# Weight tiles split ahead in attention, and activation sums by accumulating DMAs, in a hybrid decoder layer

## The chip, the cores and the metric

One Trainium2 chip, one of its cores. The metric is the device time of one launch in microseconds; the number compared is the median of runs. The engines are named as in the profile: PE (TensorE matmuls), PEld (its weight loads), DVE (VectorE), ACT (ScalarE), POOL (GpSimd) and SP (SyncE, which here only issues DMAs). Each engine works through its own instruction queue in order.

## The reference

One layer over 1024 tokens with width 1024, all in float32:

```
h = x
h = h + 0.5 * rmsnorm(swiglu(rmsnorm(h), ffn1_w_gu, ffn1_w_down))       # D_FF 2816
m = stick_breaking_attention(16 heads of 64) | mamba-2 SSD(16 heads), joined, @ w_out (2048 x 1024)
h = h + rmsnorm(m)
c = cross_attention(rmsnorm(h), 256 memory tokens, 4 heads of 256)       # wq, wkv, wo
h = h + rmsnorm(c)
h = h + 0.5 * rmsnorm(swiglu(rmsnorm(h), ffn2_w_gu, ffn2_w_down))
```

## The kernel before, in words

**Arithmetic.** Every float32 operand of a large product is split into a high part (a cast to fp32r, on ACT, line 263) and a low part (source minus high, on DVE, line 265), and each product is three matmuls: high x high, high x low, low x high (`mm3`). The tokens are two halves of 512 columns (`hh` 0 and 1), so one matmul has 128 rows and 512 columns.

**Weight tiles.** `wtile` loads a 128 x 1024 weight tile through a raw buffer (`wraw`, two of them), splits it into `whi` and `wlo` (three buffers of each tag), and for a tile named by a string such as `"q 3"` or `"out 5"` also stores both parts to DRAM (`khi`, `klo`, by POOL's queue), so that the second use loads the two parts instead of splitting again. `wstream` keeps one tile ahead. Forty-three other tiles (among them all q/k/v tiles of attention and `out 8` to `out 15`) are split during the first feed-forward by `prepare` and later loaded as `dwhi`/`dwlo`. `"out 0"` to `"out 7"` (the attention half of the output projection) are split when `mix_out` first uses them, and `"q 0"` to `"q 7"` when `xattn` first uses them.

**Stages in order.** First feed-forward up (0 to about 447 us of the profiled span) and down (`down_first`, to about 673), SSD (to about 1010), attention with the start of the output projection (to about 1578), the rest of the output projection (`mix_out`, to about 1737), cross-attention (`xattn`, to about 2000), second feed-forward.

**down_first.** The down product is done by Strassen's method: seven products (in the order 1, 5, 2, 6, 3, 7, 4) of quarter matrices, each over 11 blocks of 12 matmuls. `operands(p, b)` makes a block's left and right operands; `taker` makes them five blocks ahead of PE. Raw quarters come into a ring of four raw tiles (`wraw` and `raw2`, two each), and the split parts go to eight `hl` and eight other places. The left operands are sums of quarters of the activations A: p 5 needs A21+A22, p 6 that minus A11, p 3 A12 minus the sum of p 6, p 7 A11-A21. All 44 sums (four products x 11 blocks) are DVE additions of 128 x 512 (line 976). When a product ends, its four banks are added to the result tiles F on DVE (line 976 too), and their squares are summed for the norm (`sumsq`, two accumulators, joined by one more DVE addition on line 384).

**Order.** A planner in the framework puts the instructions of each engine in an order by simulating the program with its own durations; a tile with several buffers is given whichever buffer comes free. The order of PE is fixed by hand (each matmul behind the one before). Work beside the products hangs on `self.later`, a list keyed by a clock that counts PE's matmuls: `post` puts the norm's small matmuls (`cols`, `rows`), the eight `apply` steps of a half and its sums there; `resid` the POOL loads of the residual. Instructions from that list keep the order in which they were written on their engine.

**attention.** Eight head pairs. `inproj(p)` projects q, k and v of a pair (six products of 24 matmuls) while `units` works on the pair before: scores, a sigmoid on ACT, a scan on DVE, transposes, and products with the values. POOL does only memsets. At the end, `before` loads and scales the SSD half for the output projection, and `mix_row` makes the rows of a norm: its low tile lies in the buffer that also takes the result (`rpre1`), which the last projection still reads.

Of the kernel before, what the change touches and what calls it, by code (L numbers as in the profile page):

```python
# [18 lines left out]
P = 128  # L19
S = 1024  # L20
H = 512
KT = 8
# [24 lines left out]
class Kern:  # L47
    def __init__(self, nc, tc, ap):
        self.nc, self.tc, self.ap = nc, tc, ap
        self.uid = 0  # L50
        self.clock = 0.0
        self.prev = None
        self.floating = None
        self.pins = []
        self.later = []
        self.inlater = False
        self.more = False
        self.kept = {}

    def nm(self, base):  # L60
        self.uid += 1
# [112 lines left out]
    def wtile(self, src, eng=None):  # L174

        nc = self.nc
        key = None
        if isinstance(src, str):
            key, src = src, self.split_once(src)
        if isinstance(src, tuple):  # L180
            hi = self.t(self.wp, [P, KT, P], F32R, "whi", bufs=3)
            lo = self.t(self.wp, [P, KT, P], F32R, "wlo", bufs=3)
            for o, x in zip((hi, lo), src):
                nc.sync.dma_start(out=o.bitcast(F32), in_=x.bitcast(F32))
            return hi, lo
# [10 lines left out]
        return hi, lo  # L196

    def split_once(self, key):
        if key in self.kept:
# [138 lines left out]
        if r2 is not None:  # L338
            self.kp(nc.vector.tensor_tensor(out=c, in0=c, in1=r2, op=ALU.mult))

    def rms_rows(self, c, home, behind=False):

        nc = self.nc
        nb = c.shape[1]
        cs = self.t(self.tp, [P, 16], F32R, "cs", bufs=1)
        ch, cl = cs[:, 0:nb], cs[:, 4 : 4 + nb]
        self.kp(nc.vector.tensor_copy(ch, c))
        self.kp(nc.vector.tensor_tensor(out=cl, in0=c, in1=ch.bitcast(F32), op=ALU.subtract))
        dg = self.t(self.tp, [P, 4, P], F32R, "dg", bufs=1)
        if isinstance(home, tuple):  # L350
            pool, tag = home
            low = self.t(pool, [P, 4, P], F32R, tag, bufs=1)[:, 0:nb, :]
# [54 lines left out]
    def post(self, hh, gname, r2, gnext=None, out=None, step=None, spread=True, pins=(23000, 28000), accs=None, tail=None, times=None):  # L407
# [36 lines left out]
        def presum(d):  # L444
            if d == 0:
                accs2.extend(self.new_accs())
            self.sumsq(accs2, d, self.F[hh][d])

        T0 = self.clock
        if step is None:  # L450
            with self.pinned(T0 + t1):
                cols()
# [166 lines left out]
    def up_phase(self, sp, sp2, wgu, gpre, act_d, bank, load, plain, sizes, rw=None, begin=None, between=None):  # L619
# [162 lines left out]
        def seven(f):  # L782
# [32 lines left out]
            with self.urgent():  # L815
                nc.vector.tensor_tensor(out=t0, in0=t0, in1=b, op=ALU.mult)
            with self.urgent():
                self.emptied = nc.vector.tensor_tensor(out=e, in0=e, in1=b, op=ALU.subtract).ins  # L818
# [19 lines left out]
        def up(f, hh, t, w):  # L838
            ps = self.proj_now(w, hh)
            with self.urgent():  # L840
                nc.vector.tensor_tensor(out=t, in0=t, in1=ps, op=ALU.mult)
            store(f, hh, t)

        if begin:
# [98 lines left out]
    def seven_tools(self, sp, rw, sums_d=None):  # L943
# [31 lines left out]
        def add(o, x, y, op):  # L975
            return nc.vector.tensor_tensor(out=o, in0=x, in1=y, op=op)

        def taker(operands, ahead):
            order = [(p, b) for p in (1, 5, 2, 6, 3, 7, 4) for b in range(NFF // 2)]
            made, taken = [], [0]  # L980
# [26 lines left out]
    def down_first(self, sp, rw, wdn, act_d, gpost, gnext):  # L1007
# [10 lines left out]
            pool, tag, bufs = spot  # L1018
            return self.t(pool, [P, H], F32, tag, bufs=bufs)

        def operands(p, b):
            a, w = (lambda hh, k: act_d[b][hh][:, k, :]), (lambda k, dh: wdn[b, dh, k])
            tile = place() if p == 1 and b < 2 else self.t(sp, [P, 2, H], F32R, "hl", bufs=8)
            if p == 1:
                x, y = load(a(0, 0), w(0, 0))
                d = wdif[b] = held((self.xp, f"xl{int(b > 3)}", KT + 1))
                nc.sync.dma_start(out=d, in_=w(0, 1))
                o = parts(tile, x), parts(place(), y)
                t = wsum[b] = held(spots[b])
                i = add(t, d, y, ALU.subtract)  # L1030
                if b > 1:
                    self._after(i.ins, self.emptied)
                return o
            if p == 5:
                x, y = load(a(1, 0), a(1, 1))
                k = keep[b] = held((self.xp, f"xh{b // KT}{b % KT}", 1))
                add(k, x, y, ALU.add)
                return parts(tile, k), parts(place(), wsum[b])
            if p == 2:
                x, y = load(a(0, 1), w(1, 0))  # L1040
# [4 lines left out]
                add(wdif[b], z, wdif[b], ALU.subtract)  # L1045
                return o
            if p == 6:
                x, y = load(a(0, 0), w(1, 0))
                add(keep[b], keep[b], x, ALU.subtract)
                o = parts(tile, keep[b]), parts(place(), wsum[b])  # L1050
                add(wsum[b], wsum[b], y, ALU.subtract)
                return o
            if p == 3:
                x, y = load(a(0, 1), w(1, 1))
                add(x, x, keep.pop(b), ALU.subtract)
                return parts(tile, x), parts(place(), y)
            if p == 7:
                x, y = load(a(0, 0), a(1, 0))
                add(x, x, y, ALU.subtract)
                return parts(tile, x), parts(place(), wdif.pop(b))  # L1060
            (x,) = load(a(1, 1))
            return parts(tile, x), parts(place(), wsum.pop(b))

        take = taker(operands, 5)
        four = range(4)
        F = [[self.F[hh][4 * dh : 4 * dh + 4] for dh in range(2)] for hh in range(2)]

# [12 lines left out]
            self.more = False  # L1080

        accs = [self.new_accs(), None]

        def squares(hh, dh, i0):
            with self.urgent():
# [14 lines left out]
        ps = banks(0)  # L1100
        product(ps)
        for i in four:
            update(F[1][0][i], F[1][0][i], ps[i])
        for i in four:
            add(F[1][1][i], F[1][1][i], F[1][0][i], ALU.add)
        self.resid(0, 2700, 22000)
        ps = banks(1)
        product(ps)
# [17 lines left out]
        ps = banks(1)  # L1126
        product(ps, n=NB - 4)
        units = [take() for _ in range(4)]
        accs[1] = [held((rw, tag, 1)) for tag in ("bh", "bl")]
        squares(1, 1, 0)  # L1130
        for i in four:
            blocks(ps, units, i, False, True)
            update(F[1][0][i], F[1][0][i], ps[i], ALU.subtract)
# [518 lines left out]
    def attention(self):  # L1652
        nc, ap = self.nc, self.ap
        with self.pools("at", ["o", "a"], []) as (op, sp, pp):
# [51 lines left out]
            def inproj(p):  # L1706
# [48 lines left out]

                h0, h1 = slice(0, H), slice(H, S)
                wq = next(W)
                qevac((yield from self.proj(wq, 0)), h0)
                qevac((yield from self.proj(wq, 1)), h1)
                wk = next(W)  # L1760
                kevac(evac((yield from self.proj(wk, 0)), 0), h0)
                wv = next(W)
                tv = []
# [33 lines left out]
                    late.pop()()  # L1797

            def mix_row(i):
                product = self.rms_rows(self.norm_c[i][:, 0:4], (self.rp, f"rpre{i}"), True)  # L1800
                return lambda: self.mix_r.append(product())

            def scores(p, a, c):
# [277 lines left out]
    def xattn(self):  # L2081
# [3 lines left out]
        with self.pools("xf", ["a", "b"], []) as (sp, sp2, pp):  # L2085
# [48 lines left out]
            def values(s):  # L2134
                VH, VL = V[s]
                if s == 0:
                    self.place(sp, 128)
# [285 lines left out]
```

## Time and profile before

| | us |
|---|---|
| three runs | 2637.93, 2638.12, 2639.47 |
| median | 2638.12 |
| profiled execution | 2645.18 |
| its span, first to last instruction | 2643.4 |
| granted clock, mean over the span | 0.992 |

| engine | busy us | share of span |
|---|---|---|
| PE | 2576.9 | 97% |
| PEld | 2135.0 | 81% |
| DVE | 1983.2 | 75% |
| ACT | 1262.9 | 48% |
| POOL | 530.8 | 20% |

A row of the page that groups instructions reads: line, engine, operation, output tile <- input tiles, shapes, count, busy time, mean of one in ns, idle time of the engine just ahead of them and what ended it. A matmul's own duration overlaps the next one's; the distance of two starts is what it costs.

### The profile page before, as it was taken

The numbers are of one execution on the slowest core, as the hardware profiler recorded it, in microseconds if no ns is written. First come the engines' busy times: TensorE is split into PE (matmuls) and PEld (weight loads), VectorE is DVE, ScalarE is ACT, GpSimd is POOL, SyncE is SP. The second block draws the span as 40 slices with busy tenths as digits, with TensorE's granted clock in tenths as the row PEclk, the third lists the DMA queues.
The fourth block names the chain that finished last, engine by engine and source line by source line (L and its number), as shares of the span: only waits on it lengthen the run. The fifth ranks groups of instructions, "written<-read, shape, count | busy, mean of one in ns | idle before, by whom it ended". The sixth has DMA issues, their size and how long they took to land.

```text
span 2643.4 us, 36454 instructions
## 1 busy us (share of the span) xinstructions
PE 2576.9 (97%) x12598; PEld 2135.0 (81%) x12598; DVE 1983.2 (75%) x3085; ACT 1262.9 (48%) x2276; POOL 530.8 (20%) x660
## 2 busy tenths in 40 slices
PE   8999999999999999999999998999999999999998
PEld 6788888887777778888888787887878788888887
DVE  7888787888678774777777777775448989895675
ACT  7544443545367783445554445254445433333432
POOL 1555552001100000000000001122012555542000
PEclk9999999999999999999999999999999999999999
DMA  5688887754721226433434458777667455555976
GB/s 209 238 308 302 304 282 252 255 193 158 259 79 45 71 70 196 115 99 108 109 108 115 146 178 323 252 274 252 218 230 272 167 187 203 195 180 210 347 276 218
DMA packets 225241, 528.87 MB, mean 200 GB/s; under 512 B 28064, under 2 KB 35104, under 8 KB 225056
## 3 DMA queue, kind: packets, MB, share of 16 engines
q1 hardware_dynamic: 190432, 419.56, 48.2%
q0 software_dynamic: 27424, 93.87, 9.8%
q10 hardware_dynamic: 7200, 13.11, 1.3%
q8 instruction: 99, 1.62, 0.3%
q14 instruction: 86, 0.70, 0.1%
HBM read 353.41 MB, written 152.04 MB: 191 GB/s over the span
## 4 chain that ended last, share of the span: by engine, by line
PE 79%; DVE 9%; DMA 6%; ACT 3%; issue 2%; POOL 1%; SPq 0%; DVEq 0%; ACTq 0%; POOLq 0%
PE mm L138 45%; PE dn L138 24%; PE z L138 2%; PE ms L138 2%; PE tr L141 2%; PE y L138 1%; PE ms L141 1%; DMA wraw<-act 1%; DMA raw<-act 1%; DVE hl L265 1%; DVE wlo L265 1%; PE seg L138 1%; DMA blk<-h 1%; DVE whi L265 0%; DMA oraw<-mix 0%
## 5 line engine op out<-in xcount | busy, mean ns | idle before, releaser
L138 PE MATMUL mm<-xh,whi 128*128 128x512 f32 x1288 | 511.5, 406 | 11.1 <-ACT xh L270 7.0
L138 PE MATMUL mm<-xh,wlo 128*128 128x512 f32 x1240 | 478.5, 393 | 3.2 <-DVE wlo L265 2.9
L138 PE MATMUL mm<-xl,whi 128*128 128x512 f32 x1188 | 467.8, 394 | 1.0 <-DVE xl L265 0.7
L138 PEld LDWEIGHTS mm<-xh,whi 128*128 128x128 f32 x1288 | 244.1, 189 | 53.6 <-ACT xh L270 6.9
L138 PEld LDWEIGHTS mm<-xh,wlo 128*128 128x128 f32 x1240 | 234.3, 189 | 55.3 <-DVE wlo L265 3.4
L138 PEld LDWEIGHTS mm<-xl,whi 128*128 128x128 f32 x1188 | 225.6, 190 | 34.1 <-DVE xl L265 1.8
L1823 DVE TENSOR_TENSOR_SCAN nb<-nb,begin 128x128 f32<-128x128 f32 (+7 forms) x128 | 171.7, 1352 | 55.0 <-ACT nb L1819 54.4
L1819 ACT ACTIVATE nb<-z,scale 128x128 f32<-128x128 f32 (+2 forms) x192 | 107.8, 580 | 88.8 <-PE z L138 87.7
L263 ACT CAST whi<-wraw 128x1024 fp32r<-128x1024 f32 (+1 forms) x89 | 81.2, 914 | 69.1 <-PE mm L138 39.1
L1856 POOL MEMSET ath<- 128x128 f32 x64 | 13.1, 205 | 499.0 <-PE mm L138 499.0
L265 DVE TENSOR_TENSOR wlo<-wraw,whi 128x1024 fp32r<-128x1024 f32 x61 | 74.4, 1220 | 38.3 <-ACT whi L263 38.0
L138 PE MATMUL dn<-xh,wlo 128*128 128x512 f32 x296 | 101.0, 389 | 0.0
L737 POOL TENSOR_TENSOR wc<-wraw,raw 128x512 f32<-128x512 f32 x57 | 87.5, 1535 | 66.6 <-DVE whi L265 30.7
L737 POOL TENSOR_TENSOR wc<-raw,wraw 128x512 f32<-128x512 f32 x55 | 85.5, 1555 | 66.5 <-DVE wlo L265 31.4
L819 POOL TENSOR_TENSOR ft<-ft,e 128x512 f32<-128x512 f32 x38 | 62.4, 1642 | 144.2 <-DVE e L818 85.7
L650 ACT ACTIVATE ft<-ft 128x512 f32<-128x512 f32 x88 | 55.4, 631 | 75.0 <-DVE ft L649 70.3
L263 ACT CAST ath<-tr 128x512 fp32r<-128x512 f32 (+1 forms) x107 | 58.2, 545 | 67.5 <-PE tr L141 66.1
L138 PE MATMUL dn<-xh,blk 128*128 128x512 f32 x280 | 90.2, 389 | 0.0
L265 DVE TENSOR_TENSOR atl<-tr,ath 128x512 fp32r<-128x512 f32 (+1 forms) x107 | 67.0, 629 | 29.2 <-ACT ath L263 28.9
L138 PE MATMUL dn<-xh,whi 128*128 128x512 f32 x256 | 88.0, 389 | 0.0
L138 PE MATMUL mm<-ath,v 128*128 128x256 f32 x320 | 86.2, 291 | 0.6 <-DVE sq L1838 0.6
L382 DVE TENSOR_TENSOR acc<-acc,sq 128x512 f32<-128x512 f32 x78 | 52.3, 684 | 42.5 <-ACT sq L381 42.2
(586 smaller groups left out, 6667.9 us busy)
## 6 DMA issues: line engine op xcount, KB each, us to landing
whi<-dwhi SPq DMA_DIRECT2D x57, 512.0 KB, 3.4
wlo<-dwlo SPq DMA_DIRECT2D x57, 512.0 KB, 4.2
wraw<-act SPq DMA_DIRECT2D x102, 256.0 KB, 4.4
raw<-act SPq DMA_DIRECT2D x96, 256.0 KB, 4.3
wraw<-in_w_gu SPq DMA_DIRECT2D x44, 512.0 KB, 4.4
raw<-in_w_gu SPq DMA_DIRECT2D x38, 512.0 KB, 4.8
khi<-whi POOLq DMA_DIRECT2D x30, 512.0 KB, 4.6
klo<-wlo POOLq DMA_DIRECT2D x30, 512.0 KB, 6.7
```

The source lines that it names most:

```text
L138: self._pe(self.nc.tensor.matmul(out, lhsT, rhs, start=start, stop=stop, skip_group_check=self.more), cost)
L141: self._pe(self.nc.tensor.transpose(out, src, self.ident if ident is None else ident), 109.0)
L263: self.kp(self.nc.scalar.copy(hi, src))
L265: (eng or self.nc.vector).tensor_tensor(out=lo, in0=src, in1=hi.bitcast(F32), op=ALU.subtract)
L382: self.kp(nc.vector.tensor_tensor(out=accs[i % 2], in0=accs[i % 2], in1=sq, op=ALU.add))
L650: nc.scalar.activation(t, t, AF.Silu)
L737: nc.gpsimd.tensor_tensor(out=t, in0=a, in1=b, op=op)
L819: nc.gpsimd.tensor_tensor(out=t1, in0=t1, in1=e, op=ALU.mult)
L1819: nc.scalar.activation(nb[:, s0:s1], z[:, 0:n], AF.Sigmoid, scale=sc[:, i : i + 1])
L1823: nc.vector.tensor_tensor_scan(out=nb[:, 0:Wd][:, ::-1], data0=nb[:, 0:Wd][:, ::-1], data1=begin[:, S - Wd : S][:, ::-1], initial=0.0, op0 ...
L1856: nc.gpsimd.memset(x[:, 0, :].bitcast(F32), 0.0)
```

## The change

Two parts, which do not touch the same stages.

**Part one.** A new `split_ahead(key)` runs in `inproj(p)`: for `"q 0"` to `"q 6"` (p 1 to 7, when q's tile is taken) and for `"out 0"` to `"out 7"` (every p, when k's tile is taken). It takes a `whi` and a `wlo` buffer of the ring of three, has POOL load the raw tile into `wlo`, casts to `whi` on ACT 6500 ns of PE's clock later, subtracts in place on DVE 1000 ns after that, and stores both by POOL another 1000 ns later. `mix_out` and `xattn` then find these 15 tiles in `kept`. The low tile of the second `mix_row` moves from `rpre1` to an `ev` buffer.

**Part two.** In `down_first`, a new `fetch(p, b)` runs three blocks ahead of `operands` and forms the 44 activation sums by DMA: SP loads the first quarter into its tile, then a POOL DMA with `accum_op=ALU.add` adds the second. The up phase stores the second token half with its sign turned, so that only additions are needed, and three later updates of F change sign. In p 5, 6 and 3 the sum builds up in the `keep` tile of its block; in p 7 in a raw tile. The two sum-of-squares accumulators are no longer joined (`self.apart`): `rms_cols` takes both, at twice the small matmuls, in four places.

```diff
+    def split_ahead(self, key):
+        nc = self.nc
+        hi = self.t(self.wp, [P, KT, P], F32R, "whi", bufs=3)
+        lo = self.t(self.wp, [P, KT, P], F32R, "wlo", bufs=3)
+        raw = lo.bitcast(F32)
+        nc.gpsimd.dma_start(out=raw, in_=self.split_once(key))
...
+        def low():
+            self.kp(nc.vector.tensor_tensor(out=lo, in0=raw, in1=hi.bitcast(F32), op=ALU.subtract))
...
+        self.later += [(t + 6500, lambda: self.kp(nc.scalar.copy(hi, raw))), (t + 7500, low), (t + 8500, store)]
 ...
-        if i == KT - 1:
+        if i == KT - 1 and not self.apart:
             self.kp(nc.vector.tensor_tensor(out=accs[0], in0=accs[0], in1=accs.pop(), op=ALU.add))
 ...
+                    if fetch:
+                        while len(got) < min(len(order), len(made) + 3):
+                            got.append(fetch(*order[len(got)]))
+                        made.append(operands(*order[len(made)], got[len(made)]))
+                        continue
 ...
+        def plus(x, src):
+            nc.gpsimd.dma_start(out=x, in_=src, accum_op=ALU.add)
...
+            if p == 5:
+                k = keep[b] = held((self.xp, f"xh{b // KT}{b % KT}", 1))
+                nc.sync.dma_start(out=k, in_=a(1, 0))
+                plus(k, a(1, 1))
+                return ()
...
+            if p == 7:
+                x = load(a(0, 0))
+                plus(x[0], a(1, 0))
+                return x
...
+            x = load(w(1, int(p == 3)))
+            plus(keep[b], a(0, int(p == 3)))
+            return x
 ...
-                x, y = load(a(1, 0), a(1, 1))
-                k = keep[b] = held((self.xp, f"xh{b // KT}{b % KT}", 1))
-                add(k, x, y, ALU.add)
-                return parts(tile, k), parts(place(), wsum[b])
+                return parts(tile, keep[b]), parts(place(), wsum[b])
 ...
-            if p == 7:
-                x, y = load(a(0, 0), a(1, 0))
-                add(x, x, y, ALU.subtract)
 ...
                 wq = next(W)
+                if p:
+                    self.split_ahead(f"q {p - 1}")
 ...
                 wk = next(W)
+                self.split_ahead(f"out {p}")
```

## Rows read from the trace of the kernel before

**Rows 1.** Windows: us, then each engine's busy us (instructions), clock, DMA share, GB/s.
```profile
448.00:673.00 225.00, 216.75 (x937) 178.29 (x937) 191.45 (x313) 113.86 (x198) 17.78 (x31) 0.97 0.65 213
1600.00:1620.00 20.00, 16.34 (x68) 12.87 (x67) 14.70 (x26) 9.43 (x13) 3.60 (x7) 0.91 1.03 411
```
**Rows 2.** Waits of PE, the first down phase: total us, times, longest.
```profile
PE dn L138 <- DVE acc L384: 4.7, 1, 4.7
PE ms L138 <- DVE acc L384: 2.5, 1, 2.5
```
**Rows 3.** Windows inside the first down phase, columns as in the first group.
```profile
609.40:623.70 14.30, 8.62 (x27) 6.68 (x28) 13.80 (x28) 10.14 (x18) 0.00 (x0) 0.76 0.36 111
623.70:665.60 41.90, 41.90 (x186) 34.49 (x184) 39.66 (x64) 24.43 (x40) 9.63 (x18) 1.00 0.55 179
665.60:674.00 8.40, 5.86 (x18) 4.85 (x18) 6.09 (x11) 2.48 (x4) 1.99 (x5) 0.65 0.86 303
```
**Rows 4.** Timeline of PE and DVE there: start, us, instruction, idle before.
```profile
593.80 2.88 PE L138 MATMUL dn<-hl,whi 128*128 128x512 f32 x12
596.52 2.20 PE L138 MATMUL mm<-hl,wlo 128*128 128x512 f32 x9
...
601.24 0.69 DVE L976 TENSOR_TENSOR raw<-raw 128x512 f32<-128x512 f32 x1 [2.85 <-DMA raw<-act]
...
607.33 2.47 DVE L976 TENSOR_TENSOR F<-F,dn 128x512 f32<-128x512 f32 x4
...
679.62 0.95 PE L138 MATMUL ms<-small,bh 128*128 128x1 f32 x8
680.44 0.48 PE L138 MATMUL mm<-xl,whi 128*128 128x512 f32 x1
```
**Rows 5.** Splits of the first down phase, grouped by line and form.
```profile
L263 ACT CAST hl<-wraw 128x512 fp32r<-128x512 f32 x27 | 16.6, 619 | 26.3 <-DVE wraw L976 14.5 <-DMA wraw<-act 7.3 <-issue 1.6
L265 DVE TENSOR_TENSOR hl<-wraw,hl 128x512 fp32r<-128x512 f32 x27 | 18.4, 683 | 0.2 <-ACT hl L263 0.2
```
**Rows 6.** DMA issues, 448 to 673 us, then whole span: KB, median us to landing.
```profile
wraw<-act SPq DMA_DIRECT2D x48, 256.0 KB, 3.9
xl<-in_xT POOLq DMA_DIRECT2D x16, 256.0 KB, 5.7
...
xl<-h POOLq DMA_DIRECT2D x48, 256.0 KB, 7.7
```
**Rows 7.** Waits of PE, 1578 to 1737 us, then 1737 to 1800 us.
```profile
PE ms L138 <- DVE dg L358: 2.3, 1, 2.3
PE dn L138 <- ACT whi L263: 1.7, 1, 1.7
PE ms L138 <- DVE asum L2009: 1.4, 1, 1.4
PE dn L138 <- DVE wlo L265: 1.4, 1, 1.4
...
PE mm L138 <- DVE wlo L265: 2.9, 1, 2.9
```
**Rows 8.** Timeline of DVE ahead of the 2.3 us wait.
```profile
1606.28 1.23 DVE L265 TENSOR_TENSOR wlo<-wraw,whi 128x1024 fp32r<-128x1024 f32 x1 [1.92 <-ACT whi L263]
...
1609.37 1.19 DVE L265 TENSOR_TENSOR wlo<-wraw,whi 128x1024 fp32r<-128x1024 f32 x1
```
**Rows 9.** Splits of weight tiles, 1737 to 1791 us, grouped by line and form.
```profile
L265 DVE TENSOR_TENSOR wlo<-wraw,whi 128x1024 fp32r<-128x1024 f32 x6 | 7.3, 1218 | 2.3 <-ACT whi L263 2.3
L263 ACT CAST whi<-wraw 128x1024 fp32r<-128x1024 f32 x5 | 5.3, 1056 | 3.8 <-PE mm L138 3.0 <-ACT acc L378 0.7
```
**Rows 10.** One period of attention and a stretch of cross-attention, columns as in the first group.
```profile
1160.00:1180.00 20.00, 19.20 (x119) 16.68 (x118) 17.45 (x27) 10.89 (x23) 1.04 (x6) 1.00 0.42 133
1180.00:1200.00 20.00, 20.00 (x112) 17.18 (x111) 15.04 (x17) 10.37 (x20) 0.79 (x5) 1.00 0.46 114
1760.00:1780.00 20.00, 20.00 (x106) 16.89 (x106) 19.76 (x46) 13.96 (x30) 5.66 (x11) 1.00 0.84 286
```

More of the change, by code (lines that the diff above doesn't have):

```diff
@@ L196, in wtile, with store @@
         return hi, lo
+    def split_ahead(self, key):
[4 more added lines that the diff above has]
+        nc.gpsimd.dma_start(out=raw, in_=self.split_once(key))
+        hl = self.kept[key] = tuple(self.tc.dram_tile([P, KT, P], F32R, name=self.nm(n)) for n in ("khi", "klo"))
+        def low():
+            self.kp(nc.vector.tensor_tensor(out=lo, in0=raw, in1=hi.bitcast(F32), op=ALU.subtract))
+        def store():
+            for d, x in zip(hl, (hi, lo)):
+                self.kp(nc.gpsimd.dma_start(out=d.bitcast(F32), in_=x.bitcast(F32)))
+        t = self.clock
+        self.later += [(t + 6500, lambda: self.kp(nc.scalar.copy(hi, raw))), (t + 7500, low), (t + 8500, store)]
     def split_once(self, key):
@@ L339, in rms_cols, with rms_rows @@
             self.kp(nc.vector.tensor_tensor(out=c, in0=c, in1=r2, op=ALU.mult))
-    def rms_rows(self, c, home, behind=False):
+    def rms_rows(self, c, home, behind=False, at=None):
         nc = self.nc
@@ L351, in rms_rows @@
             pool, tag = home
-            low = self.t(pool, [P, 4, P], F32R, tag, bufs=1)[:, 0:nb, :]
+            low = self.t(at or pool, [P, 4, P], F32R, "ev" if at else tag, bufs=2 if at else 1)[:, 0:nb, :]
         else:
@@ L446, in presum @@
                 accs2.extend(self.new_accs())
+            self.apart = apart
             self.sumsq(accs2, d, self.F[hh][d])
+            self.apart = False
         T0 = self.clock
+        apart, self.apart = self.apart, False
         if step is None:
@@ L817, in seven @@
             with self.urgent():
-                self.emptied = nc.vector.tensor_tensor(out=e, in0=e, in1=b, op=ALU.subtract).ins
+                x, y = (b, e) if begin else (e, b)
+                self.emptied = nc.vector.tensor_tensor(out=e, in0=x, in1=y, op=ALU.subtract).ins
             nc.gpsimd.tensor_tensor(out=t1, in0=t1, in1=e, op=ALU.mult)
@@ L840, in up @@
             with self.urgent():
-                nc.vector.tensor_tensor(out=t, in0=t, in1=ps, op=ALU.mult)
+                if begin and hh:
+                    nc.vector.scalar_tensor_tensor(out=t, in0=t, scalar=-1.0, in1=ps, op0=ALU.mult, op1=ALU.mult)
+                else:
+                    nc.vector.tensor_tensor(out=t, in0=t, in1=ps, op=ALU.mult)
             store(f, hh, t)
@@ L976, in add, with taker @@
             return nc.vector.tensor_tensor(out=o, in0=x, in1=y, op=op)
-        def taker(operands, ahead):
+        def taker(operands, ahead, fetch=None):
             order = [(p, b) for p in (1, 5, 2, 6, 3, 7, 4) for b in range(NFF // 2)]
-            made, taken = [], [0]
+            made, taken, got = [], [0], []
             def take():
@@ L1019, in held, with sources, fetch, operands @@
             return self.t(pool, [P, H], F32, tag, bufs=bufs)
-        def operands(p, b):
-            a, w = (lambda hh, k: act_d[b][hh][:, k, :]), (lambda k, dh: wdn[b, dh, k])
+        def sources(b):
+            return (lambda hh, k: act_d[b][hh][:, k, :]), (lambda k, dh: wdn[b, dh, k])
+        def plus(x, src):
+            nc.gpsimd.dma_start(out=x, in_=src, accum_op=ALU.add)
+        def fetch(p, b):
+            a, w = sources(b)
+            if p == 1:
+                d = wdif[b] = held((self.xp, f"xl{int(b > 3)}", KT + 1))
+                x = load(a(0, 0), w(0, 0))
+                nc.sync.dma_start(out=d, in_=w(0, 1))
+                return x
[4 more added lines that the diff above has]
+                return ()
+            if p == 2:
+                return load(a(0, 1), w(1, 0))
+            if p == 7:
+                x = load(a(0, 0))
+                plus(x[0], a(1, 0))
+                return x
+            if p == 4:
+                return load(a(1, 1))
+            x = load(w(1, int(p == 3)))
+            plus(keep[b], a(0, int(p == 3)))
+            return x
+        def operands(p, b, got):
+            a, w = sources(b)
             tile = place() if p == 1 and b < 2 else self.t(sp, [P, 2, H], F32R, "hl", bufs=8)
             if p == 1:
-                x, y = load(a(0, 0), w(0, 0))
-                d = wdif[b] = held((self.xp, f"xl{int(b > 3)}", KT + 1))
-                nc.sync.dma_start(out=d, in_=w(0, 1))
+                x, y = got
                 o = parts(tile, x), parts(place(), y)
                 t = wsum[b] = held(spots[b])
-                i = add(t, d, y, ALU.subtract)
+                i = add(t, wdif[b], y, ALU.subtract)
                 if b > 1:
@@ L1034, in operands @@
             if p == 5:
-                x, y = load(a(1, 0), a(1, 1))
-                k = keep[b] = held((self.xp, f"xh{b // KT}{b % KT}", 1))
-                add(k, x, y, ALU.add)
-                return parts(tile, k), parts(place(), wsum[b])
+                return parts(tile, keep[b]), parts(place(), wsum[b])
             if p == 2:
-                x, y = load(a(0, 1), w(1, 0))
+                x, y = got
                 z = self.t(*((self.tp, [P, H], F32, "dg", 1) if b % 2 else (self.fp, [P, H], F32, "rpost", 1)))
@@ L1047, in operands @@
             if p == 6:
-                x, y = load(a(0, 0), w(1, 0))
-                add(keep[b], keep[b], x, ALU.subtract)
                 o = parts(tile, keep[b]), parts(place(), wsum[b])
-                add(wsum[b], wsum[b], y, ALU.subtract)
+                add(wsum[b], wsum[b], got[0], ALU.subtract)
                 return o
             if p == 3:
-                x, y = load(a(0, 1), w(1, 1))
-                add(x, x, keep.pop(b), ALU.subtract)
-                return parts(tile, x), parts(place(), y)
-            if p == 7:
-                x, y = load(a(0, 0), a(1, 0))
-                add(x, x, y, ALU.subtract)
[L1060 to L1064, printed above, removed]
+                return parts(tile, keep.pop(b)), parts(place(), got[0])
+            return parts(tile, got[0]), parts(place(), (wdif if p == 7 else wsum).pop(b))
+        take = taker(operands, 5, fetch)
         four = range(4)
@@ L1102, in down_first @@
         for i in four:
-            update(F[1][0][i], F[1][0][i], ps[i])
+            update(F[1][0][i], F[1][0][i], ps[i], ALU.subtract)
         for i in four:
-            add(F[1][1][i], F[1][1][i], F[1][0][i], ALU.add)
+            add(F[1][1][i], F[1][0][i], F[1][1][i], ALU.subtract)
         self.resid(0, 2700, 22000)
@@ L1799, in mix_row @@
             def mix_row(i):
-                product = self.rms_rows(self.norm_c[i][:, 0:4], (self.rp, f"rpre{i}"), True)
+                product = self.rms_rows(self.norm_c[i][:, 0:4], (self.rp, f"rpre{i}"), True, sp if i else None)
                 return lambda: self.mix_r.append(product())
@@ L2136, in values @@
                 if s == 0:
-                    self.place(sp, 128)
+                    self.place(sp, 384)
                 pT = [[self.t(sp, [P, H], F32R, f"pt{n}{m}", bufs=1) for m in range(2)] for n in range(2)]
```

5 lines of the change are left out of this document (4 added, 1 removed).

## The prediction

> **What bounds the kernel now.** I read the engines' busy shares first: PE 97%, DVE 75%, ACT 48%, POOL 20%. A kernel whose matmul engine is that full can gain only where PE stands still or runs at a lowered clock, so I went on to the windows by stage and, in the stages that the change touches, to PE's waits. PE is idle for 225.00 - 216.75 = 8.3 us of the first down phase and for 3.7 of 20 us in `mix_out` [rows 1], but for only 0.8 us in one of attention's full thirds and for none in the next [rows 10]. A removed DVE or ACT instruction is worth nothing by itself; it is worth the PE wait that it stood in front of, and the slow matmuls behind that wait. The full-speed price of a 512-column matmul is (596.52 - 593.80) / 12 = 0.227 us, start to start [rows 4].
>
> In the first down phase PE waits twice, both times for the joining addition of the squares (line 384), 4.7 and 2.5 us [rows 2]. The window of the first wait lasts 14.30 us at a granted clock of 0.76 and holds 27 matmul records: 8 small ones and 19 of 512 columns [rows 3]. At full speed they need 0.82 us (680.44 - 679.62 for eight small ones [rows 4]) + 19 x 0.227 = 5.1 us, so the stop costs 9.2 us with the half-speed matmuls behind it. The second window, 8.40 us with 18 records, needs 0.82 + 10 x 0.227 = 3.1 and costs 5.3 us [rows 3].
>
> Why DVE is late is seen in the timeline: PE has done product 3 at 596.52, but the additions of its banks to F start at 607.33 [rows 4]. In between DVE does blocks of product 7 that the planner put ahead of F, and stands idle, 2.85 us in one place, at the head of its queue for raw activations still on their way [rows 4]. DVE is late by 10.8 us because transfers land later than the planned order needs.
>
> In `mix_out` PE waits 1.7 and 1.4 us for the two parts of an `out` tile, 1.4 for a sum of squares, 2.3 for the rows of a norm; in `xattn` 2.9 for the low part of a `q` tile [rows 7].
>
> **Part one, term by term.** It takes 15 splits out of `mix_out` and `xattn`, each 1.22 us of DVE and 1.06 of ACT [rows 9], with two 512 KB stores each on POOL's queue; the tiles are then loaded as two parts.
> (a) The waits for the parts of an `out` tile: -3.1 us. Both parts then come by DMA, with nothing of ACT or DVE ahead; the DMAs are full in that stretch, a share of 1.03 [rows 1], but a raw load and two stores become two loads, so there is a third less traffic for these tiles.
> (b) The 2.3 us wait: two low splits of 1.23 and 1.19 us stand on DVE ahead of it [rows 8], and without them the rows come 2.4 us earlier. The window around it holds 68 records at a granted clock of 0.91 [rows 1]: 8 small and 60 of 512 columns need 14.4 of the 20 us, 5.6 are lost, 1.4 and 2.3 of them in waits [rows 7], 1.9 in slow matmuls. The 1.4 us wait for the sum of squares stays; with the slow matmuls, -2.3 - 1.9 = -4.2 us.
> (c) The 2.9 us wait is for `q 7`, the one q tile that isn't split ahead. But five of the six low splits ahead of it go, 5 x 1.22 = 6.1 us of a DVE that is 19.76/20 busy there [rows 9, 10]. The wait and slow matmuls behind it, 1.9 us as in (b), are 4.8; as `q 7` keeps some place in the planned order, I take three quarters: -3.6 us.
> (d) What attention pays: 15 x (1.22 + 1.06) us of DVE and ACT, 15 POOL loads and 30 stores. Per head pair (about 57 us) that is two splits; DVE is 17.45/20 busy in the last third and 15.04/20 in the next [rows 10], and the splits fall, by their due times, into the first two thirds. PE's order is not changed. From below it costs 0, since ACT and DVE have idle time in which PE's work is already queued; from above every low split stands once in front of PE, 15 x 1.22 = 18.3 us. I take +2, near the lower end, because PE loses only 0.8 us of 20 even in the fullest third [rows 10]. Queued behind a cast that waits for its POOL load are the sigmoids and the casts of the transposes, for which PE waits next. POOL has only memsets in this stage. The three-buffer ring carries one more tile; v's tile must wait until q's is done, about two products before it is needed. The low tile in `ev` I cost at nothing, since both `ev` buffers are also busy at that time.
> Together: -3.1 - 4.2 - 3.6 + 2 = -8.9 us.
>
> **Part two, term by term.** It takes 44 x 0.68 = 30 us of additions and the waits ahead of them off DVE, and adds 44 accumulating POOL DMAs.
> (e) The first stop, 9.2 us. F's additions come in time if the blocks of product 7 that stand ahead of them land in time. A block's raw tile is now held through an SP load (3.9 us), POOL's wait and issue (0.54), the accumulating DMA, the cast (0.62) and the subtraction (0.68) [rows 5, 6]. No row shows an accumulating DMA. Its nearest rows are plain POOL loads of the same size, 5.7 us and over the whole span 7.7 [rows 6]. It might land no later than a plain SP load, 3.9; twice the slower POOL row is 15.4. I take 5.7, the row of this stage. The hold is then 11.4 us; four raw tiles give a block every 2.9 us against PE's 2.72, and the up to eight blocks of lead hide the difference. About seven blocks of product 7 are planned ahead of F, and fetching for it starts three blocks (8.2 us) into product 3: the second round of four lands 8.2 + 11.4 + 10.1 = 29.7 us into a product of 29.9, so F starts some 2 us behind PE in place of 10.8. I take -7 of the 9.2.
> (f) The second stop, 5.3 us: DVE is 39.66/41.90 busy between the two [rows 3], and 11 of the additions that went were in product 7, 7.5 us. But post's eight `apply` steps and the splits stay. I take -2.
> (g) The small matmuls: four places, eight more records each, 4 x 0.82 = +3.3 us on PE, which nothing hides; the four joining additions of 0.68 that go are in (e) and (f).
> The other 33 sums (products 5, 6, 3) have a tile of their own for each block and 21 us of lead; PE is full there now, so they bring nothing and cost nothing as long as load and accumulation take under 21 us. The sign changes keep counts and shapes, but for three multiplications of another form.
> Together: -7 - 2 + 3.3 = -5.7 us.
>
> By the Trainium skill's page "DMA: Bandwidth & Descriptors", section "Rules for kernel authors", an accumulating DMA must wait for the semaphore of the earlier DMA on the same bytes: the two latencies add up, as in the hold above. Its section on the SWDGE path gives 2.0 us + bytes / 436 GB/s, 2.6 us for 256 KB; the hold would be 7.0 and F would be on time. The rows are slower, 5.7 to 7.7, so I stay with them.
>
> **Sum.** -8.9 - 5.7 = -14.6 us of the profiled execution's 2645.18, all in stretches that a normal run has as well. The median run is 7.1 us shorter than that execution, which the profile doesn't explain; I carry the difference over unchanged: 2638.1 - 14.6 = 2623.5 us.
>
> **Rivals.** 1. *The accumulation is late and the stop stays.* If it lands in 9 us instead of 5.7, the hold is 14.7 and F starts 8 us late: the first stop remains, (e) and (f) bring nothing, (g) is still paid: 2638.1 - 8.9 + 3.3 = 2632.5. For it: DVE's queue is in order and already 10.8 us late through one DMA, now there are two in a row. Against: three blocks more of lead.
> 2. *Slower: product 7 starves.* At 15.4 us the hold is 21.1. Four raw tiles start 8.2 us into product 3; blocks 4 to 7 land 8.2 + 21.1 + 19.8 = 49 us into it, while PE wants block 4 at 40.8: 8 us of standstill, and blocks 8 to 10 another 10. With (a) to (d) and (g): 2638.1 - 8.9 + 3.3 + 18 = 2650.5. It decides from a landing of about 9 us on, where blocks 4 to 7 pass 36 us and use up the lead.
> 3. *Attention gives part one back.* The casts wait for POOL loads, or the splits fall in the full third: (d) is 10 instead of 2: 2623.5 + 8 = 2631.5; with rival 1 as well, 2632.5 + 8 = 2640.5. For it: PE already waits for DVE in that third. Against: the DMAs are busy only 0.42 to 0.46 there [rows 10].
> 4. *The planner re-orders and the change does not do what it says:* the waits of (b) and (c) move to other instructions and only (a) and (e) remain: 2638.1 - 3.1 + 2 - 7 + 3.3 = 2633.3.
>
> **Chances.** Forecast 0.45 (own range 2616 to 2631), rival 1 0.19, rival 2 0.12, rival 3 0.14 (a third of it together with rival 1), rival 4 0.10. A measurement of this kernel can't tell less than about 0.2%, 5.3 us, from no change: faster is below 2632.8, slower above 2643.4. Rivals 1 and 4 lie on the edge, half on either side; of rival 3 half is faster. Faster 0.45 + 0.10 + 0.07 + 0.05 = 0.67; slower is rival 2 and a little of rival 3, 0.15; the rest 0.18. The range of 8 in 10 is 2613 to 2643: at its lower end both stops of the down phase and all of (c) go.
>
> **What would show it.** The changed profile should have, between 596 and 625 us, F's additions within 3 us of the end of product 3 and no PE wait over 1 us; 16 small records in place of 8 at four places; no casts of 128 x 1024 in `mix_out`; and 15 more pairs of cast and subtraction in attention with PE's idle time there up by 2 us or less. The time from an accumulating DMA's issue to its landing decides between the forecast and rivals 1 and 2. The prediction is wrong if PE stands still in product 7, or if PE's idle time in attention grows by as much as it falls later.

## The result: slower, and the profile after

The changed kernel takes 2653.5 us (median of four runs, 2648.6 to 2655.6) where the kernel before, on the same chip, took 2638.8. The ratio is 1.0050 (95% interval 1.0038 to 1.0062), so 13 us slower by the ratio and 14.7 by the medians. 2623.5 us was forecast, in a range of 2613 to 2643.

The engines' busy times from the page of the changed kernel:

```profile
PE 2583.9 (97%) x12614; PEld 2140.8 (81%) x12614; DVE 1952.9 (74%) x3039; ACT 1262.4 (48%) x2276; POOL 577.6 (22%) x719
```

This line says little: DVE has less work, and PE's share is the same. The windows tell more (columns as in [rows 1]); behind them stands one of the kernel before:

```profile
448.00:673.00 225.00, 213.15 (x929) 175.51 (x929) 158.75 (x258) 109.59 (x193) 49.51 (x65) 0.97 0.72 193
440.00:460.00 20.00, 19.32 (x86) 15.66 (x84) 11.07 (x18) 4.80 (x8) 7.54 (x9) 1.00 1.07 301
460.00:480.00 20.00, 11.36 (x39) 9.16 (x40) 10.86 (x18) 9.58 (x18) 4.05 (x5) 0.74 0.91 248
```
```profile
440.00:480.00 40.00, 40.00 (x177) 32.85 (x176) 31.57 (x51) 18.51 (x33) 4.84 (x7) 1.00 0.74 246
```

In the first down phase DVE fell from 191.45 to 158.75 us busy, as meant, and yet PE works 3.6 us less of the same 225 than in [rows 1]. Where the phase begins, at 460 to 480 us, PE has 39 records in 20 us, at a clock of 0.74; in the kernel before it was busy for all of 440 to 480 us. There it did 177 matmuls in these 40 us and here 125; at 0.227 us each the missing 52 are an estimated 11.8 us, nearly the whole loss. PE's waits (total us, times, longest), first at 440 to 480 us, then at 600 to 720:

```profile
PE dn L139 <- ACT dx L284: 9.3, 1, 9.3
...
PE dn L139 <- DVE dg L379: 2.5, 1, 2.5
PE ms L139 <- DVE rpre L379: 2.2, 1, 2.2
PE ms L139 <- DVE acc L403: 0.7, 1, 0.7
PE ms L139 <- DVE dg L379: 0.5, 1, 0.5
```

The two waits for `acc` of [rows 2], 4.7 and 2.5 us, became 0 and 0.7. The waits for the norms' rows (`dg`, `rpre`), the next link of the same chain, grew from 0.9 and 0.6 us (too short for [rows 2]) to 2.5 and 2.2, and a stop of 9.3 us is new. The chain of waits shows what released it (start, us, what):

```profile
447.11 11.04 DMA xh<-act
...
459.56 0.61 POOL ft L844
...
460.64 0.53 POOL xh L1058
...
461.21 6.70 DMA act<-ft
...
467.97 0.63 ACT dx L284
...
468.64 6.55 PE dn L139 x17
```

Read from below: PE waits for a cast of ACT into `dx`. That cast waits for the store of `ft`, the up phase's last activation. The store waits for POOL's multiplication at line 844, and that stands in POOL's queue behind eight accumulating DMAs of product 5 (line 1058), each of which waits for the load into the same `xh` tile. POOL's timeline has the multiplication in the changed kernel and then in the kernel before, 10.9 us apart:

```profile
459.25 1.60 POOL L844 TENSOR_TENSOR ft<-ft,e 128x512 f32<-128x512 f32 x1
```
```profile
448.39 1.61 POOL L819 TENSOR_TENSOR ft<-ft,e 128x512 f32<-128x512 f32 x1 [16.56 <-issue]
```

The DMAs of 448 to 470 us (per queue: packets, MB, share of 16 engines' span; q0 holds POOL's DMAs, q1 SP's), and then two of SP's loads in the same window of the kernel before:

```profile
q0 software_dynamic: 1376, 2.62, 61.9%
q1 hardware_dynamic: 1476, 2.68, 35.0%
...
xh<-act POOLq DMA_DIRECT2D x7, 256.0 KB, 6.6
xh<-act SPq DMA_DIRECT2D x2, 256.0 KB, 12.3
wraw<-act SPq DMA_DIRECT2D x2, 256.0 KB, 7.3
...
raw<-in_w_dn SPq DMA_DIRECT2D x1, 256.0 KB, 10.2
```
```profile
raw<-act SPq DMA_DIRECT2D x6, 256.0 KB, 4.7
...
wraw<-in_w_dn SPq DMA_DIRECT2D x2, 256.0 KB, 7.3
```

The two queues move nearly the same megabytes, but the accumulating one takes 0.619 x 22 x 16 / 2.62 = 83 us of engine time per MB and SP's 46. The engines are full, and SP's loads land after 7 to 12 us where the kernel before had 4.7 to 7.3.

### The profile page after: what moved, and what is told of

The parts are those of the page before. It is cut to its first block, busy times and chain, and to the rows that moved or that the text cites. A ratio compares the mean times of both kernels' runs of the same rounds, so it can differ in the third digit from the quotient of the medians.

```text
span 2653.8 us, 36560 instructions
## 1 busy us (share of the span) xinstructions
PE 2583.9 (97%) x12614; PEld 2140.8 (81%) x12614; DVE 1952.9 (74%) x3039; ACT 1262.4 (48%) x2276; POOL 577.6 (22%) x719
## 4 chain that ended last, share of the span: by engine, by line
PE 80%; DVE 7%; DMA 5%; issue 4%; ACT 2%; POOL 1%; SPq 0%; DVEq 0%; ACTq 0%; POOLq 0%
PE mm L139 43%; PE dn L139 27%; PE ms L139 2%; PE z L139 2%; PE tr L142 1%; PE y L139 1%; PE ms L142 1%; DMA wlo<-klo 1%; PE seg L139 1%; DVE nb L1877 1%; DMA raw<-act 1%; DMA blk<-h 0%; PE st L139 0%; DVE atl L286 0%; DMA xh<-act 0%
## 5 line engine op out<-in xcount | busy, mean ns | idle before, releaser
L284 ACT CAST whi<-wraw 128x1024 fp32r<-128x1024 f32 (+1 forms) x77 | 67.4, 876 | 53.5 <-PE mm L139 40.2
L139 PE MATMUL mm<-atl,v 128*128 128x256 f32 x320 | 82.7, 280 | 0.1
```

The lines of the kernel that those rows point to most:

```text
L139: self._pe(self.nc.tensor.matmul(out, lhsT, rhs, start=start, stop=stop, skip_group_check=self.more), cost)
L284: self.kp(self.nc.scalar.copy(hi, src))
```

## The experiments

Each ratio is to the kernel before on the same chip, with its 95% interval; 0.001 is 2.6 us. A trace is one execution: the changed kernel and part_two below have the same instructions in the same order up to 1010 us, and yet the small matmuls of the phase's last norm start at 733.5 us in one trace and at 726.5 in the other, so a microsecond or two in a single trace proves nothing. The theory at the start (T): the loss is the start of the first down phase.

**1. part_one.** The kernel before with the hunks of part one (`split_ahead` and its two calls, the diagonal in `ev`, `place` of 384) and nothing else.
```
+                if p:
+                    self.split_ahead(f"q {p - 1}")
...
+                self.split_ahead(f"out {p}")
...
-                    self.place(sp, 128)
+                    self.place(sp, 384)
```

> The kernel before with part one alone (out and q tiles split during attention, mix_row's low diagonal in a buffer of the phase's own pool). Theory T (the loss is in the first down phase: accumulating DMAs stand in POOL's queue ahead of the up phase's last multiplication and store, and load the DMA engines): 2636, from 2632 to 2640, since the gains of part one stand in the changed kernel's trace (4 us at 1760 to 1800, 3.6 at 1560 to 1600) against losses of 2.5 at 1480 to 1520, 1.7 at 1720 and 3.5 at 1000 to 1040. Rival A (attention pays for the split tiles and the 15.7 MB more that they move): 2642 to 2650, most of the 14.7 us that were lost.

Measured: 2646.1 us, 1.0016 (1.0004 to 1.0028). The time lies in rival A's range and not in T's. By the ratio part one costs 4 us by itself, which T had not, but that is not most of the loss, as rival A had it.

**2. part_two.** The changed kernel without those hunks.
```
-                if p:
-                    self.split_ahead(f"q {p - 1}")
...
-                self.split_ahead(f"out {p}")
...
-                    self.place(sp, 384)
+                    self.place(sp, 128)
```

> The changed kernel without part one: only the first feed-forward's accumulating DMAs, the signs and the separate squares. Theory T: 2653, from 2648 to 2657, the whole loss, with the same stop of 9 us before the first down phase at about 460 and the second at 683. Rival A (attention pays): 2630 to 2640.

Measured: 2651.2 us, 1.0042 (1.0029 to 1.0055), 11 of the 13 us, with a stop for `dx` of 9.8 us. T holds for the larger part.

**3. behind_store.**
```
-            nc.gpsimd.dma_start(out=act_d[f // 2][1][:, f % 2, :], in_=t1)
+            self.laststore = nc.gpsimd.dma_start(out=act_d[f // 2][1][:, f % 2, :], in_=t1).ins
...
-            nc.gpsimd.dma_start(out=x, in_=src, accum_op=ALU.add)
+            self._after(nc.gpsimd.dma_start(out=x, in_=src, accum_op=ALU.add).ins, self.laststore)
```


> The changed kernel with one order added on POOL's queue: every accumulating DMA behind the up phase's last multiplication and store. PE's, DVE's, ACT's and SP's instructions keep their order. Theory T in its strict form (the place in the queue): the stop at 460 falls from 9.3 us to under 2, and the time to 2645, from 2642 to 2648. Rival B (the accumulating DMAs fill the DMA engines, whose share was 0.99 there, wherever they stand in the queue): the stop stays at 6 us or more, now as a wait for a load, and the time at 2650 to 2656.

Measured: 2647.6 us, 1.0031 (1.0020 to 1.0041), some 5 us off the changed kernel. POOL's timeline (start, us) and the DMA issues of 448 to 470 us (KB, median us to landing):

```profile
450.55 1.61 POOL L844 TENSOR_TENSOR ft<-ft,e 128x512 f32<-128x512 f32 x1 [16.90 <-issue]
...
453.03 8.14 POOL L1058 DMA_DIRECT2D xh<-act  x9
```
```profile
xh<-act POOLq DMA_DIRECT2D x11, 256.0 KB, 13.7
raw<-act SPq DMA_DIRECT2D x3, 256.0 KB, 12.5
raw<-in_w_dn SPq DMA_DIRECT2D x3, 256.0 KB, 14.2
```
The multiplication is 8.7 us earlier and the wait for `dx` is gone, so the queue's order was one cause. But the accumulations now come in one bunch, loads land after 12 to 14 us, and PE loses time all the same (1.3 us of 460 to 480 in waits for parts). The time is in T's range; rival B's full engines hold a share.

**4. joined.** The changed kernel, its squares joined on DVE again (at two places).
```
-        self.apart = True
```

> The changed kernel with the two sums of squares joined by an addition on DVE again, so without the 14 additional small matmuls. Theory T: 2650 to 2656, the stops at 460 and 683 stay. Rival C (the small matmuls cost more than the 3.3 us forecast for them and lower the clock): 2640 to 2648.

Measured: 2652.8 us, 1.0048 (1.0031 to 1.0066), like the changed kernel: the additional small matmuls (sixteen in the trace) are not the loss (rival C falls). Their price is below what the runs tell apart.

**5. plain_copies.** Line 1058 of the changed kernel, for the sums of all four products, which this kernel leaves out.
```
-            nc.gpsimd.dma_start(out=x, in_=src, accum_op=ALU.add)
+            nc.gpsimd.dma_start(out=x, in_=src)
```

> The changed kernel with the additions taken out of the accumulating DMAs: the same transfers between the same tiles in the same places of the queues, as plain copies, so the sums of activations and weights of the first feed-forward are left out. Theory T2 (the stop at 460 is the place in POOL's queue and the transfer before it that each accumulation waits for, with the DMA engines full because an accumulating packet takes them twice as long): the packets of the second queue take about 0.08 us in place of 0.16, the stop falls from 9.3 to 3 to 6 us, and the time to 2645 to 2650. Rival D (the accumulation costs no more than a copy, and only the order of the queue counts): the stop stays at 8 to 10 us and the time at 2651 to 2656.

Measured: 2644.8 us, 1.0007 (0.9996 to 1.0017): 11 us of the 13 are gone. DMA queues of 448 to 470 us, then PE's wait:

```profile
q1 hardware_dynamic: 2255, 4.11, 55.7%
q0 software_dynamic: 770, 2.50, 29.8%
```
```profile
PE dn L139 <- ACT dx L284: 3.2, 1, 3.2
```
As many megabytes from the same queue now take 0.298 x 352 / 2.50 = 42 us of engine time per MB, half of the accumulations' 83, and the stop is in T2's range; rival D falls. T2 expected half the time for each packet; in fact the packets are fewer and larger, and it is the megabyte that costs half.

**6. five_on_dve.** part_two with product 5's sums on DVE:
```
             if p == 5:
-                k = keep[b] = held((self.xp, f"xh{b // KT}{b % KT}", 1))
-                nc.sync.dma_start(out=k, in_=a(1, 0))
-                plus(k, a(1, 1))
-                return ()
+                return load(a(1, 0), a(1, 1))
...
+                k = keep[b] = held((self.xp, f"xh{b // KT}{b % KT}", 1))
+                add(k, *got, ALU.add)
...
```


> Part two alone (as part_two, 2651), with the eleven sums of product 5 made by DVE again out of two loads into the ring; products 7, 6 and 3 keep their accumulating DMAs. Theory T2 (the loss of part two is product 5's accumulations behind the up phase): no stop at 460, and 10 to 12 us off part_two: 2640, from 2636 to 2643. Rival E (the accumulations cost as much in products 6, 3 and 7, by the load of the DMA engines): no stop at 460, but 2645 or more.

Measured: 2639.7 us, 0.9993 (0.9982 to 1.0005), 13 us off part_two. PE in 440 to 480 us:

```profile
440.00:480.00 40.00, 40.00 (x177) 32.85 (x176) 33.09 (x53) 20.19 (x35) 7.44 (x8) 1.00 0.74 224
```
No stop. Product 5's eleven accumulations alone are the whole loss of part two; the 33 that are left cost nothing that can be measured, and rival E falls.

**7. five_pins.** five_on_dve with other due times for the first norm (its call, shortened).
```
-self.post(0, ..., step=4700, ..., times=(12000, 15500, 17500), tail=(5500, 9000))
+self.post(0, ..., step=4300, ..., times=(12000, 18500, 20000), tail=(4500, 10000))
```

> five_on_dve with the first norm of the down phase moved in the plan: its rows 3 us later behind its columns (18.5 us for 15.5), and the steps behind them accordingly. Theory F (the stop at 609 went on to the next link of the same chain, since the diagonal of the norm's rows stands behind four splits in DVE's queue): the wait of 2.2 to 2.5 us for dg at about 628 goes under 0.5, and the time falls by 2 to 4 us against five_on_dve. Rival G (the stop only moves on once more, to the later link): no difference, within 1.5 us.

Measured: 2640.6 us, 0.9987 (0.9976 to 0.9998): not apart from five_on_dve. The wait for `dg` fell from 1.7 to 1.2 us, and at the second stop 4.5 us for `acc` appeared where it had been 0.7. Rival G: the stop goes on.

**8. q_only.** part_one without the out tiles.
```
-                self.split_ahead(f"out {p}")
```

> Part one alone (as part_one, 2646), without the tiles of the out projection: only the q tiles are split during attention. Theory H (each split tile's loads and stores lengthen the row copies into k and q that attention waits for, and the out tiles give nothing back, since their wait for DVE has become a wait for a DMA): the gain at 1770 stays (4 us), the loss at 1040 to 1100 falls from 6 to 3 us or less, and the time to 2638, from 2635 to 2641. Rival I (what part one costs is the q tiles, or the moved diagonal and the buffers): 2643 to 2648.

Measured: 2637.5 us, 0.9983 (0.9974 to 0.9991): 4.5 us faster than the kernel before, and 0.33% or 8.7 us under part_one. PE's waits of 1040 to 1110 us in part_one, SP's of 1040 to 1070, and the row copies into `k` of 1040 to 1064:

```profile
PE z L138 <- DMA k<-xl: 2.6, 1, 2.6
...
SPq L184 <- DMA khi<-whi: 4.4, 1, 4.4
```
```profile
k<-xl SPq DMA_DIRECT2D x4, 128.0 KB, 5.3
```
The same copies in q_only:
```profile
k<-xl SPq DMA_DIRECT2D x4, 128.0 KB, 2.5
```
And the window of 1040 to 1110 us, in part_one and then in q_only:
```profile
1040.00:1110.00 70.00, 65.34 (x341) 54.95 (x340) 46.67 (x61) 31.94 (x57) 6.36 (x20) 0.98 0.57 168
```
```profile
1040.00:1110.00 70.00, 69.62 (x377) 58.94 (x376) 47.72 (x66) 30.69 (x59) 3.69 (x15) 1.00 0.48 142
```
SP's next weight load waits 4.4 us until the split tile's store has left its buffer of the ring. So SP's last weight load ahead of the row copies starts at 1054.29 us in place of 1049.11, and it is still on its way, with POOL's load of the next raw tile, when the row copies into `k` are issued (at 1056.56, and in q_only at 1057.35). They land after 5.3 us in place of 2.5, and PE waits for them: 341 records in place of 377. This is read from the two traces; no run takes the ring's wait away alone. What q_only gains is the `q 7` wait: PE is busy for all 40 us of 1760 to 1800, where it was 37.05 in the kernel before. H holds and rival I falls.

**9 and 10. combo** (q_only's and five_on_dve's edits on the changed kernel) **and combo_pins** (the same with five_pins' times).

> Both parts with their two costs taken out: q tiles split during attention and not the out tiles (as q_only), and products 7, 6 and 3 with accumulating DMAs but the sums of product 5 on DVE (as five_on_dve). Theory T2 with H (the two parts lie 300 us apart and do not touch): the gains add, 0.9983 by 0.9993, so 0.9976 of the time before, 2634 against 2640; range 0.996 to 0.999. Rival (they meet, through the order that the planner makes): not faster than q_only, 0.9983 or more.

> combo with the first norm's rows 3 us later in the plan (as five_pins). Theory G (the stop only goes on to a later link, as the 4.5 us for acc in five_pins show): within 0.06% of combo. Rival F: 0.1% or more under combo.

Measured: 0.9985 (0.9976 to 0.9993) and 0.9977 (0.9968 to 0.9985). By its point combo is not faster than q_only, as the rival had it; by the intervals the two can't be told apart, nor can combo_pins from combo. Whether the gains add stays open.

**11. combo_urgent.** combo with the norms' columns and rows of this phase in the planner's higher priority:
```
+        def first(f):
+            with self.urgent() if soon else ExitStack():
+                f()
+
-        q = [(t1, cols), (t2, rows)]
+        q = [(t1, lambda: first(cols)), (t2, lambda: first(rows))]
...
```


> combo with the columns and rows of the two norms of the first down phase raised in the planner's priority, so that they stand ahead of the splits that were emitted before them. If the stops of 2.2 us at 628 and 1.5 + 2.2 us at 680 are DVE's queue (theory F2), they fall by 3 us or more and the time by 0.1% against combo; if the splits that are put behind them are then late for their matmuls (rival), no gain, or a loss.

Measured: 2632.5 us, 0.9963 (0.9952 to 0.9975). The second norm's waits (0.4 and 2.2 us in combo, where the diagonal of `rpre` stood on DVE at 675.73 us behind a split that had waited for ACT) are gone. The first norm's remains; PE's wait, then the timeline of PE and DVE:

```profile
PE dn L139 <- DVE dg L379: 3.7, 1, 3.7
```
```profile
611.72 1.84 PE L139 MATMUL dn<-small,acc 128*128 128x1 f32 x16
...
613.93 0.69 DVE L286 TENSOR_TENSOR hl<-wraw,hl 128x512 fp32r<-128x512 f32 x1 [3.19 <-ACT hl L284]
...
618.81 0.15 DVE L353 TENSOR_TENSOR cpost<-dn,cpre 128x4 f32<-128x4 f32 x1
```
The columns are done at 613.6, but DVE takes them at 618.81: ahead of them in its queue stand splits of product 7, for which it stood idle 3.19 us, and ACT, which casts for them, had itself waited 3.34 us for raw activations still on their way. F2 is right for the second stop; the first is a transfer.

**12. seven_on_dve.** combo_urgent with
```
             if p == 7:
-                x = load(a(0, 0))
-                plus(x[0], a(1, 0))
-                return x
+                return load(a(0, 0), a(1, 0))
...
+            if p == 7:
+                add(got[0], *got, ALU.add)
```


> combo_urgent (0.9963) with product 7's eleven sums on DVE too, so that only products 6 and 3 are left with accumulating DMAs. In combo_urgent PE still waits 3.7 us for dg at about 617, since DVE stands 3.2 us at a product 7 split whose raw activations have not landed. Theory J (the second transfer in a row, 5 to 7 us, holds those raw tiles too long): that wait falls to 1 us or less and the time by 0.1% or more. Rival K (the eleven additions of 0.68 us put DVE behind instead, as in the kernel before): a wait of 3 us or more stays at 600 to 630, and the time is within 0.1% of combo_urgent or above it.

Measured: 2628.9 us, 0.9958 (0.9945 to 0.9972), the fastest of all, 11 us under the kernel before. The wait for `dg` fell from 3.7 us to none. PE's only wait of 440 to 720 us, the phase's window and the timeline at the first norm:

```profile
PE ms L139 <- DVE acc L403: 0.7, 1, 0.7
```
```profile
448.00:673.00 225.00, 224.32 (x995) 185.78 (x994) 182.91 (x306) 116.73 (x203) 37.56 (x54) 0.98 0.72 220
```
```profile
609.71 1.84 PE L139 MATMUL dn<-small,acc 128*128 128x1 f32 x16
...
611.76 0.16 DVE L353 TENSOR_TENSOR cpost<-dn,cpre 128x4 f32<-128x4 f32 x1
...
613.17 0.68 DVE L379 TENSOR_TENSOR dg<-ident,cs 128x512 fp32r<-128x512 f32 x1
...
615.14 0.39 PE L139 MATMUL dn<-dg,onesr 128*128 128x512 f32 x1
```
The rows are there 1.3 us before PE wants them. Theory J holds in the trace; in the time its step of 0.05%, where 0.1% was expected, is within the intervals.

## Why the prediction was wrong

**The step that failed** is "The other 33 sums (products 5, 6, 3) have a tile of their own for each block and 21 us of lead; PE is full there now, so they bring nothing and cost nothing". For product 5 they cost 0.49% or 12.9 us (part_two less five_on_dve); for products 6 and 3 no cost could be measured. The test in that step, load and accumulation under 21 us, was even met by the two transfers: 12.3 + 6.6 = 18.9 us. With the wait in POOL's queue between them two of the eleven took longer than 21 us, but PE waited for none of these sums. It was the wrong test: it asked when the sums are ready, and not what stands behind them. On POOL's queue that was the up phase's last multiplication with its store, for which the first cast into `dx` waited; on the DMA engines it was every load of the phase's first blocks. Ahead of that store POOL's queue had held nothing but work of the up phase, and the prediction asked only in attention what else stands in it. Experiments 3, 5 and 6 show the shares, which overlap and are uncertain by 4 to 5 us: the order 5 us, the accumulation in place of a copy up to 11 (taken from all four products), both together 13.

**(e), (f), the two stops, -9 forecast.** Without product 5, part two is worth 0.07% or 1.9 us with an interval that includes nothing, where -5.7 was forecast. The landing was sized well (5.7 us taken, 5.1 and 7.2 us measured for product 7's two kinds of raw tile between 560 and 625 us), and so was F. Timeline of the changed kernel, PE's first matmuls of product 7 and then F's additions:

```profile
609.90 2.20 PE L139 MATMUL mm<-hl,wlo 128*128 128x512 f32 x9
...
612.95 2.47 DVE L1004 TENSOR_TENSOR F<-F,dn 128x512 f32<-128x512 f32 x4
```
F starts 3.0 us behind the end of product 3, where 10.8 had been and 2 was forecast; in five_on_dve it is 2.7. But the stop was priced as if nothing came after F: the norm's columns and rows stand behind product 7's splits in DVE's queue, and those wait for the second transfer (without it, in experiment 12, the wait is gone). So the waits of 600 to 720 us fell only from 8.7 us to 5.9, and to 6.5 in five_on_dve. It is rival 1's pair of transfers in a row on DVE's in-order queue, but it holds up what comes behind F and not F itself, and at a shorter landing than the 9 us that rival 1 was given. Rival 2's standstill in product 7 did not appear.

**(g)** Sixteen small matmuls take 1.84 us where eight took 0.95 [rows 4], as forecast for one place. But the trace has sixteen in two places only, at 622.60 and 674.96 us; in the other two there are eight, as before:

```profile
691.01 1.70 PE L139 MATMUL ms<-small,bh 128*128 128x1 f32 x8
```
Two of the four joining additions are still there, so the kernel does not do what was said of it in four places: by its code, a step of the first half's sums that runs between the second half's squares sets `apart` back. (g) was therefore worth about 1.8 us and not 3.3, an estimate from these durations; taking the sixteen away changed nothing that can be measured.

**(a), (b), the out tiles.** The waits for ACT and DVE went, and waits for DMAs came. PE's waits of 1560 to 1740 us in the changed kernel, largest first:

```profile
PE dn L139 <- DMA whi<-khi: 2.6, 1, 2.6
PE dn L139 <- DMA wlo<-klo: 2.4, 3, 1.2
```
Against [rows 7] PE waits 5.0 us for the two parts of `out` tiles where it waited 3.1, so (a) has the wrong sign; less traffic did not help. The waits of (b), 2.3 and 1.4 us, are gone. The out tiles together cost 8.7 us, most of it in attention: its last scan starts 6.2 us later in part_one than in q_only (timelines of DVE, in this order).

```profile
1568.60 2.29 DVE L1846 TENSOR_TENSOR_SCAN nb<-nb,begin 128x1024 f32<-128x1024 f32 x1
```
```profile
1562.41 2.28 DVE L1845 TENSOR_TENSOR_SCAN nb<-nb,begin 128x1024 f32<-128x1024 f32 x1
```

**(c)** Right: the `q 7` wait of 2.9 us is gone, and PE is full from 1760 to 1800 us in q_only. The q tiles are worth 4.5 us where (c) had 3.6.

**(d)** +2 was forecast from DVE and ACT being idle there. The price was paid elsewhere: by SP's loads, which wait for a ring buffer until a store has left it, and by row copies that land late. This is near rival 3's outcome (10 us in place of 2), for the out tiles, by a way that the text named only as one more tile in the ring. After product 5 it is the second step that failed: (a), (b) and (d) together had the out tiles as a gain.

By ratios, the four shares are +12.9 (product 5), -1.9 (the rest of part two), +8.7 (out tiles) and -4.5 (q tiles); their sum, 15, agrees with the 13 measured, since each is uncertain by 2 to 5 us. The forecast had 0 and -5.7 for the first two, and -8.9 for the last two together, which came to +4.2.

## What to carry to other kernels

An accumulating DMA, as used here, takes work off one engine and puts a wait into POOL's queue: list what stands behind that wait and whose buffer depends on it, before asking whether the sum itself is early enough. Work moved ahead in a ring can be paid with the time for which its stores hold the ring's buffers. Where a wait goes, follow the same chain one link on, through each in-order queue, until it reaches something that is early.

## What the runs showed of the hardware

In the window of 448 to 470 us a megabyte took the DMA engines 83 us in accumulating DMAs, 42 in plain copies at the same place of the queue, and 46 to 48 in SP's copies. The same holds in product 3, at 532 to 556 us, where POOL's queue has these DMAs alone, in the changed kernel and then in plain_copies:

```profile
q0 software_dynamic: 1008, 1.84, 47.0%
```
```profile
q0 software_dynamic: 707, 2.31, 29.5%
```
That is 0.470 x 24 x 16 / 1.84 = 98 us per MB against 49. There it cost PE nothing: in the changed kernel it is busy for all 120 us of 480 to 600.

The accumulating DMA of 256 KB landed after 6.4 us in the median of its 33 issues of product 5, 6 and 3, and after 13.7 us where eleven came together. The Trainium skill, "DMA: Bandwidth & Descriptors", section "Anatomy of one DMA — SWDGE (gpsimd) path", fits 2.0 us + bytes / 436 GB/s; worked out for this size, that is an estimate of 2.6 us, less than half of the shorter of these medians, so the measurement decides. After the 9.3 us stop the granted clock of the window 460 to 480 us was 0.74; in the window of the first stop of [rows 3] it was 0.76.
